# Four column groups of an output projection as seven block products each, with the heads' operand sums kept in DRAM

## The chip, the cores and the metric

The kernel runs on one core of a Trainium2 chip. TensorE (PE) multiplies 128x128 weight tiles with operands of up to 512 columns and adds up in PSUM. VectorE (DVE), ScalarE (ACT) and GpSimd (POOL) work beside it on SBUF and PSUM. Transfers are issued by SyncE (SP) and by POOL, each on a queue of its own that is worked off in order, and carried by the core's 16 DMA engines. The metric is the device time of one execution in microseconds, the median of three runs: 2347.07 us before the change (2345.48 to 2347.75).

## The reference

One layer of a hybrid streaming encoder on 512 prompt frames and 32 sample frames (T = 544 columns here, since the kernel keeps features on partitions). What matters:

```python
x   = layer_norm(x) @ w_in                      # 2048 -> 4928
o_h = rms_norm(hgrn2_recurrence(q, 1 - f, log f, i)) * silu(g)    # 8 heads of 128
o_a = mla_attention(...)                                          # 8 heads of 128
out = concat([o_h, o_a]) @ w_out                # 2048 -> 2048
h   = layer_norm(ALPHA * h + out)
ff  = (silu(conv(h @ w_up)) * (h @ w_gate)) @ w_down
y   = layer_norm(ALPHA * h + ff)
```

Everything is float32.

## The kernel before, in words

**Products.** A float32 product is made from three products of rounded parts: each weight tile is split into a high part `wh` (ACT, a copy to the rounded type) and a low part `wl = raw - wh` (DVE), each operand likewise into `aH` and `aL`, and PE adds wh·aH, wh·aL and wl·aH (`mm3`). A matmul has 128 rows, 128 columns of weight and 272 columns of operand: T is halved into columns 0 to 271 (j = 0) and 272 to 543 (j = 1). A weight piece is 128x1024 (512 KB): four 128-row blocks by 256 output columns. It serves 48 matmuls when both halves of T are done, 24 for one half.

**Seven products.** Where a matrix product is cut into 2x2 blocks, the kernel can form it from seven block products in place of eight (`ORDER`: 11, s1, s2, s4, s3, 12, 22), with sums of weight blocks as weights and sums of operand blocks as operands. The later two thirds of the input projection (class `Divided`, L788) and the feed-forward layer (classes `Blocks` and `Item`, played by `play`, L1257 and L1288) are done so. `play` walks a list of items: it multiplies item n, splits the weights of item n+2 (`prep`) and forms the weight sum of item n+3 (`form`); the result of item n-1 is added from PSUM in its `sink`.

**Around the change.** In order of time: the attention heads (`attend`, results into DRAM tiles `cat_dr`); the recurrence of eight heads woven into the divided input projection (`levels(h)` and `finish(h)`, which ends in the head's output `o`); then `out_first`, which loads and splits all 16 heads into `cH`, `cL` and makes output columns group 0 (256 columns) as a plain product while the last head is finished; then groups 1 to 4 as plain products of both halves (`gemm`, 192 matmuls each); groups 5 and 6 with half 0 only (`gemm_half`, 96 matmuls each); group 7's half 0 and half 1 of groups 7, 5 and 6 in `step`, with the first norm's work between the steps (`TASKS`).

**The first norm.** `h0` (the normalised input) is loaded back from DRAM into `za` (features 0 to 7, on POOL's queue) and `zb` (8 to 15, on SP's queue). `z = ALPHA * z + product`. Behind group 0 `Norm.first` takes a first estimate of the row means, for each half j: DVE `n_e = za0 + za1`, PE sums of one column (`sums`), DVE `nt_c`, PE spreads them over the partitions (`spread`), ACT `n_cb`. From then on every block of z is made as ALPHA*z - cb (`shifted`) and has the product added (`joined`); row sums and sums of squares are carried along (POOL `n_s`, ACT `n_e`, DVE `n_s`).

**Order.** Inside `manual_schedule` blocks each engine's order is the program's. The part from `finish` of the last head to group 6 is not in such a block: there the framework decides the order of the instructions of each engine from its own estimate of when they can run. Pools give out buffers in rings (`raw` three, `wh` and `wl` four), and a buffer is written again when its readers are through.

Of the kernel before, what the change touches and what calls it, by code (L numbers as in the profile page):

```python
# [9 lines left out]
I32 = mybir.dt.int32  # L10
# [36 lines left out]
HK = 8  # L47
# [12 lines left out]
def tile_encoder_step(ctx, tc, xp, xs, w_in, w_in4, w_kr, w_q_b, w_kv_b, w_out, w_up, w_gate, w_down, w_down2,  # L60
# [14 lines left out]
    cat_dr = [dram.tile([P, 2, T], F32, name=f"catd{k}", tag=f"catd{k}") for k in range(KD // 2)]  # L75

# [17 lines left out]

    def load_raw(src, kc, ncols):
        raw = wp.tile([P, 1024], F32, name="raw", tag="raw", bufs=3)[:, :kc * ncols]
        dma(raw, src)
        return raw.rearrange("p (k c) -> p k c", k=kc)
# [49 lines left out]
    def pair_half(ps, j):  # L148
        n = H_[j].stop - H_[j].start
        return [ps[:, 512 * t:512 * t + n] for t in range(2)]  # L150

# [46 lines left out]
    with tc.tile_pool(name="p0", bufs=1) as p0, tc.tile_pool(name="ps0", bufs=4, space=PSUM) as ps0:  # L198
# [12 lines left out]
        def load_first(kk):  # L211
            for g in range(2):
                raws[kk, g] = p0.tile([P, 4, 256], F32, name="raw0", tag="raw0", bufs=5) if g or kk == 3 else \
                    wp.tile([P, 1024], F32, name="raw", tag="raw", bufs=3).rearrange("p (k c) -> p k c", k=4)
# [149 lines left out]
    with tc.tile_pool(name="mp", bufs=1) as mp, tc.tile_pool(name="psa", bufs=4, space=PSUM) as psa:  # L364
# [208 lines left out]
        def attend(pr):  # L573
# [58 lines left out]
            dma(cat_dr[4 + pr], o)  # L632

# [8 lines left out]
    def out_piece(kk, g):  # L642
        return piece(w_out[kk, g], 4, 256)
# [12 lines left out]
    with tc.tile_pool(name="gp", bufs=1) as gp, tc.tile_pool(name="psg", bufs=1, space=PSUM) as psg:  # L656
        hm = gp.tile([P, T + 272 * 6], I32, name="hm")
# [19 lines left out]
        def sums_of_inputs():  # L677

            load_sums()
            for k in range(HK):  # L680
# [9 lines left out]
                V.tensor_tensor(out=a, in0=t0, in1=t1, op=ALU.subtract)  # L690
                V.tensor_tensor(out=b, in0=t1, in1=t1b, op=ALU.add)
                V.tensor_tensor(out=c, in0=b, in1=t0, op=ALU.subtract)
# [3 lines left out]
                V.tensor_tensor(out=a, in0=t0b, in1=c, op=ALU.subtract)  # L696
# [8 lines left out]

        class Divided:


            def __init__(self, c):
                self.c, self.raw = c, {}  # L710

            def load(self, key):
                if key == "21":
                    self.raw[key] = gp.tile([P, HK * P], F32, name="raw21", tag="raw21")
                else:
                    self.raw[key] = wp.tile([P, 1024], F32, name="raw", tag="raw", bufs=3)
                dma(self.raw[key], w_in4[self.c - N_PLAIN, int(key[0]) - 1, int(key[1]) - 1])

            def form(self, name):
                if name == "11":  # L720
                    for key in ("11", "12", "22", "21"):
                        self.load(key)
                r = self.raw
# [619 lines left out]
    for name in ("11", "12"):  # L1343
        open_op(name, apx, "right")
# [1047 lines left out]
```

## Time and profile before

| | us |
|---|---|
| median of three runs | 2347.07 |
| the profiled execution, its own time | 2347.67 |
| span of its trace | 2345.9 |
| PE busy in the span | 2305.4 |
| mean granted clock of PE | 0.994 |

| stage | from, to (us of the span) |
|---|---|
| divided input projection with the recurrence | 383 to 701 |
| output columns group 0 | 701.4 to 730.4 |
| groups 1 to 4 | 730.4 to 832 |
| groups 5 and 6, half 0 | 832 to 856.5 |
| group 7, halves 1, first norm | 856.5 to 907 |
| feed-forward layer and last norm | 907 to 2346 |

How to read the rows: an engine's row in a timeline has its start, its length, the engine, the line of the kernel, the operation, the tile written and the tiles read, and in brackets how long the engine was idle before it and what released it. A table of stretches gives for each engine the busy time and the number of instructions, then PE's granted clock (1.00 is full), the busy share of the DMA engines and what they moved. A DMA row gives the number of transfers, KB of each and the median time from issue to landing.

### The profile page before, as it was taken

The numbers are of one execution on the slowest core, as the hardware profiler recorded it, in microseconds if no ns is written. First come the engines' busy times: TensorE is split into PE (matmuls) and PEld (weight loads), VectorE is DVE, ScalarE is ACT, GpSimd is POOL, SyncE is SP. The second block draws the span as 40 slices with busy tenths as digits, with TensorE's granted clock in tenths as the row PEclk, the third lists the DMA queues.
The fourth block names the chain that finished last, engine by engine and source line by source line (L and its number), as shares of the span: only waits on it lengthen the run. The fifth ranks groups of instructions, "written<-read, shape, count | busy, mean of one in ns | idle before, by whom it ended". The sixth has DMA issues, their size and how long they took to land.

```text
span 2345.9 us, 44466 instructions
## 1 busy us (share of the span) xinstructions
PE 2305.4 (98%) x18340; PEld 2289.3 (98%) x18340; DVE 1703.1 (73%) x2357; ACT 1075.3 (46%) x1652; POOL 221.4 (9%) x277
## 2 busy tenths in 40 slices
PE   7999999999999999999999999999999999999996
PEld 6999999999999999999999999999999999999996
DVE  7455578777786358987777777777777677777776
ACT  5345434433352227665555554555555433333323
POOL 1010000000001111000010000100001111111102
PEclk9999999999999999999999999999999999999998
DMA  6332263222245236777677676776777999889832
GB/s 238 104 99 84 69 205 104 86 93 82 81 144 194 91 109 210 217 203 207 201 179 227 176 198 208 176 230 177 190 216 190 371 325 303 270 277 299 286 94 79
DMA packets 155963, 427.47 MB, mean 182 GB/s; under 512 B 14192, under 2 KB 70256, under 8 KB 148464
## 3 DMA queue, kind: packets, MB, share of 16 engines
q1 hardware_dynamic: 129488, 302.20, 37.4%
q0 software_dynamic: 26272, 122.43, 21.8%
q8 instruction: 144, 2.36, 0.4%
q14 instruction: 59, 0.48, 0.1%
HBM read 351.75 MB, written 70.11 MB: 180 GB/s over the span
## 4 chain that ended last, share of the span: by engine, by line
PE 95%; DVE 1%; ACT 1%; DMA 1%; issue 1%; POOL 0%; ACTq 0%; SPq 0%; DVEq 0%
PE main L1257 22%; PE acc L1257 17%; PE main L118 13%; PE main L788 11%; PE main L1288 11%; PE acc L1288 7%; PE acc L118 5%; PE s L853 2%; PE main L555 1%; PE at L616 1%; PE at L585 1%; DMA x<-in_xp 1%; PE main L542 0%; PE at L587 0%; DMA raw<-in_w_in 0%
## 5 line engine op out<-in xcount | busy, mean ns | idle before, releaser
L1199 DVE TENSOR_TENSOR wl<-raw,wh 128x1024 fp32r<-128x1024 f32 x353 | 431.9, 1223 | 192.5 <-ACT wh L1198 192.2
L1198 ACT ACTIVATE wh<-raw 128x1024 fp32r<-128x1024 f32 x353 | 373.2, 1059 | 388.0 <-PE main L1257 99.2
L1257 PE MATMUL main<-op,wh 128*128 128x272 f32 x1408 | 265.4, 287 | 0.0
L1257 PE MATMUL acc<-ops,wh 128*128 128x272 f32 x1344 | 254.1, 287 | 0.0
L1257 PE MATMUL main<-ops,wh 128*128 128x272 f32 x1344 | 254.1, 287 | 0.0
L1257 PEld LDWEIGHTS main<-op,wh 128*128 128x128 f32 x1408 | 221.0, 188 | 0.0
L1257 PEld LDWEIGHTS acc<-ops,wh 128*128 128x128 f32 x1344 | 211.1, 188 | 0.0
L1257 PEld LDWEIGHTS main<-ops,wh 128*128 128x128 f32 x1344 | 211.0, 188 | 0.0
L1257 PE MATMUL main<-op,wl 128*128 128x272 f32 x704 | 202.9, 288 | 0.3 <-DVE wl L1199 0.3
L1257 PE MATMUL main<-ops,wl 128*128 128x272 f32 x672 | 193.7, 288 | 0.0
L1257 PE MATMUL acc<-ops,wl 128*128 128x272 f32 x672 | 193.7, 288 | 0.0
L118 PE MATMUL main<-aH,wh 128*128 128x272 f32 (+2 forms) x736 | 176.5, 296 | 0.2 <-ACT wh L280 0.2
L118 PE MATMUL main<-aH,wl 128*128 128x272 f32 (+2 forms) x736 | 172.7, 291 | 1.8 <-DVE wl L281 1.8
L118 PE MATMUL main<-aL,wh 128*128 128x272 f32 (+2 forms) x736 | 172.3, 291 | 1.0 <-DVE aL L269 1.0
L1257 PE MATMUL acc<-op,wh 128*128 128x272 f32 x832 | 157.5, 288 | 1.0 <-ACT ea L1511 1.0
L1198 ACT ACTIVATE wh<-rawl 128x1024 fp32r<-128x1024 f32 x93 | 98.9, 1063 | 118.4 <-PE acc L1257 45.8
L107 DVE TENSOR_TENSOR wl<-raw,wh 128x1024 fp32r<-128x1024 f32 (+2 forms) x72 | 80.2, 1117 | 89.6 <-ACT wh L106 85.6
L732 ACT ACTIVATE wh<-raw 128x1024 fp32r<-128x1024 f32 x84 | 88.7, 1056 | 111.4 <-DVE raw L727 105.1
L1199 DVE TENSOR_TENSOR wl<-rawl,wh 128x1024 fp32r<-128x1024 f32 x93 | 113.8, 1223 | 27.7 <-ACT wh L1198 27.6
L1257 PEld LDWEIGHTS main<-op,wl 128*128 128x128 f32 x704 | 132.2, 188 | 0.5 <-DVE wl L1199 0.5
L1257 PEld LDWEIGHTS acc<-op,wh 128*128 128x128 f32 x832 | 130.4, 188 | 1.2 <-ACT ea L1511 1.2
L1257 PEld LDWEIGHTS main<-ops,wl 128*128 128x128 f32 x672 | 126.3, 188 | 0.0
(448 smaller groups left out, 5998.0 us busy)
## 6 DMA issues: line engine op xcount, KB each, us to landing
raw<-in_w_in SPq DMA_DIRECT2D x76, 512.0 KB, 3.6
raw<-in_w_up SPq DMA_DIRECT2D x71, 512.0 KB, 4.9
raw<-in_w_gate SPq DMA_DIRECT2D x71, 512.0 KB, 4.8
raw<-in_w_down SPq DMA_DIRECT2D x67, 512.0 KB, 9.4
opd<-ohl SPq DMA_DIRECT2D x20, 1088.0 KB, 5.5
ops<-opd POOLq DMA_DIRECT2D x20, 1088.0 KB, 12.0
raw<-in_w_out SPq DMA_DIRECT2D x40, 512.0 KB, 3.6
raw<-in_w_up POOLq DMA_DIRECT2D x35, 512.0 KB, 5.3
```

What stands on the lines that cost most here:

```text
L107: V.tensor_tensor(out=dst(lv), in0=src(rv), in1=dst(hv).bitcast(F32), op=ALU.subtract)
L118: PE.matmul(ps, ww[:, wcols[0]:wcols[1]], aa[:, hs[j]], start=first and i == 0, stop=last and i == 2, skip_group_check=True)
L555: PE.matmul(ps[:, j * 512:j * 512 + 256], l[k][:, a:b], r4(w[:, k:k + 1, :])[:, 0, :, 128:256], start=k == 0 and i == 0, stop=k == 1 and i ...
L585: PE.matmul(sc[:, :nk], qn[j][:, q0:q0 + P], kn[j][:, :nk], start=True, stop=False)
L616: PE.matmul(po[:, :P], vt[:, k, j, :], t[:, k * P:(k + 1) * P], start=k == 0, stop=k == b)
L732: A.activation(wh, self.src, AF.Copy)
L788: PE.matmul(out, ww[:, k * P:(k + 1) * P], aa, start=name in ("11", "s1", "12") and k == 0 and q == 0, stop=k == HK - 1 and q == 2, skip_g ...
L853: PE.matmul(ps[:, j * 64:(j + 1) * 64], Kp[:, a:b], Qv[:, j * bt:(j + 1) * bt, 1, :], start=True, stop=True)
L1198: A.activation(wh, src, AF.Copy)
L1199: V.tensor_tensor(out=wl, in0=src, in1=wh.bitcast(F32), op=ALU.subtract)
L1257: PE.matmul(ps, ww[:, k * P:(k + 1) * P], aa, start=self.first and k == 0 and i == 0, stop=k == n - 1 and i == 2, skip_group_check=True)
L1288: PE.matmul(banks[:, 512 * u:512 * u + NI], ww[:, (u * n + k) * P:(u * n + k + 1) * P], aa, start=self.first and k == 0 and i == 0, stop=k ...
```

## The change

Output column groups 1 to 4 (features 256 to 1279) become seven block products each, from weights that are laid out in 2x2 blocks (`w_out4`). A block has 1024 rows by 128 columns, so one product is 24 matmuls, and the four groups are 28 items of class `Out`. They are played by `play`, first products 11 and 12 of all four groups, then for each group s1, s2, s4, s3, 22.

The operands of 11, 12 and 22 are halves of the heads themselves (`cH`, `cL`). Those of s1, s2, s3 and s4 are sums over pairs of a recurrence head and an attention head. `finish(h)` forms them for its head, while the recurrence runs, in high and low parts, and stores them in DRAM (`ou_dr`, four stores of 278 KB for each head); for that `attend` leaves the difference of its output's halves in DRAM (`d3_dr`). s1, s2 and s4 are loaded back into `su` (six loads of 1088 KB on POOL's queue). s3 is placed over the second halves of the attention heads in `cH`, `cL` (`place_s3`), after these have been copied to DRAM (`a21_dr`, 16 stores on POOL's queue); they are loaded back behind the last s3 product (`place_a21`, 16 loads on SP's queue).

The order of the groups changes: group 0, then groups 5 and 6 half 0, then the 28 items, then group 7 as before.

In the recurrence `Divided` makes its weight sums by two DVE additions and two accumulating DMAs on POOL's queue for each group, where there were four DVE subtractions; the signs of the operand sums and of the results change with that. The mask `hm` becomes 8-bit. Buffers `raw` have tags of their own.

```diff
@@ finish, behind the head's output o
+            hl = {}
+            def high(name, x):
+                hl[name] = gp.tile([P, 2, NI], R, name="hl", tag="hl", bufs=2)
+                A.activation(hl[name][:, 0], x, AF.Copy)
+            def low(name, x):
+                V.tensor_tensor(out=hl[name][:, 1], in0=x, in1=hl[name][:, 0].bitcast(F32), op=ALU.subtract)
+                dma(ou_dr[name][h // 4][:, :, h % 4], hl[name].bitcast(F32))
+            yield
+            minus(ab[:, 0], o[:, NI:], ab[:, 0])
+            high("s3", ab[:, 1])
+            yield
+            low("s3", ab[:, 1])
+            high("s1", ab[:, 0])
+            opposite(ab[:, 1], ab[:, 1], o[:, NI:])
...
+            low("s4", ab[:, 1])
@@ Divided
             def form(self, name):
-                        V.tensor_tensor(out=r[out], in0=r[a], in1=r[b], op=ALU.subtract)
+                if name in ("s1", "s2"):
+                    other = {"s1": "12", "s2": "22"}[name]
+                    V.tensor_tensor(out=self.t("11"), in0=self.t("11"), in1=self.t(other), op=ALU.add)
+                if name == "s1":
+                    G.dma_start(self.t("12"), self.src("22"), accum_op=ALU.add)
             def low(self, wh):
+                if self.name == "s2":
+                    G.dma_start(self.t("11"), self.src("21"), accum_op=ALU.add)
+                elif self.name not in ("11", "s1"):
+                    slots.append(self.raw.pop(self.key)[0])
+                    supply()
@@ out_first, split_cats
+                    if k >= HK:
+                        for n, t in enumerate((cH[k], cL[k])):
+                            G.dma_start(a21_dr[k - HK][:, n], t[:, NI:].bitcast(F32))
@@ behind the loads of za and zb
+    for n in ("s1", "s2", "s4"):
+        for i in range(2):
+            G.dma_start(su[n][i].bitcast(F32), ou_dr[n][i])
@@ groups
-    for g in range(1, 5):
-        tiles = [acc_tile(), acc_tile()]
-        run(gemm(tiles, lambda kk: out_piece(kk, g), cact, CAT_ORDER))
...
-    for g in (5, 6, 7):
+    for g in (5, 6):
...
+    class Out(Item):
+        def operand(self, k):
+            if self.name in su:
+                return [su[self.name][k // 4][:, i, k % 4] for i in range(2)]
+            kg, j = {"11": (HK + k, 0), "12": (k, 0), "22": (k, 1), "s3": (HK + k, 1)}[self.name]
+            return cH[kg][:, H_[j]], cL[kg][:, H_[j]]
+        def multiply(self):
+            wh, wl = self.w
+            for k in range(HK):
+                oh, ol = self.operand(k)
+                for i, (ww, aa) in enumerate(((wh, oh), (wh, ol), (wl, oh))):
+                    PE.matmul(self.bank, ww[:, k * P:(k + 1) * P], aa, start=self.first and k == 0 and i == 0,
+                              stop=k == HK - 1 and i == 2, skip_group_check=True)
...
+        def out_sink(g, name, ps):
+            t, j = PLACE[name]
+            z = zt[2 * g + t][:, H_[j]]
+            if (g, t, j) in touched:
+                V.tensor_tensor(out=z, in0=z, in1=ps, op=SIGN[t])
+            else:
+                touched.add((g, t, j))
+                V.scalar_tensor_tensor(out=z, in0=z, scalar=ALPHA, in1=ps, op0=ALU.mult, op1=SIGN[t])
+            if name in ("s4", "22"):
+                close_rows(g, 0 if name == "s4" else 1)
...
+        for g in range(1, 5):
+            for name, key, bank in (("11", "11", X[g]), ("12", "21", BC[g % 2])):
+                oitems.append(out_item(out_blocks(g, (key,)), g, name, bank, True))
+        for g in range(1, 5):
+            b = out_blocks(g, ("11", "12", "22"))
+            oitems += [out_item(b, g, name, BC[(g + 1) % 2] if name in ("s1", "s4") else X[g])
+                       for name in ("s1", "s2", "s4", "s3", "22")]
...
+        ohooks = {0: [lambda: place_s3(range(4))], 1: [lambda: place_s3(range(4, 8))],
+                  NO - 2: [lambda: split_seventh(0)],
+                  NO - 1: [place_a21, lambda: split_seventh(1), lambda: [shifted(14 + t, 0) for t in range(2)]]}
+        play(oitems, 0, ohooks)
```

Since the framework orders this place anew, here are the rows of three engines there, before and with the change.

DVE, from the last head's output (`og`, split into `aL`) to the first norm's second half, before:

```order
L177 TENSOR_TENSOR aL<-og,aH 128x544
L1397 SCALAR_TENSOR_TENSOR za<-za,main 128x272 x4
L1059 TENSOR_TENSOR n_e<-za 128x272
L107 TENSOR_TENSOR wl<-raw,wh 128x1024
L1065 TENSOR_SCALAR nt_c<-main 128x3
L1076 TENSOR_TENSOR za<-za,n_cb_8319 128x272
L1077 TENSOR_TENSOR za<-za,n_cb_8319 128x272
L1356 SCALAR_TENSOR_TENSOR za<-za,n_cb_8319 128x272 x2
L1086 SCALAR_TENSOR_TENSOR n_s_8322<-n_e 128x272
L1356 SCALAR_TENSOR_TENSOR za<-za,n_cb_8319 128x272
L1059 TENSOR_TENSOR n_e<-za 128x272
```

With the change:

```order
L991 TENSOR_TENSOR hl<-ab,hl 128x272 x2
L167 SCALAR_TENSOR_TENSOR ab<-ab,og 128x272
L118 TENSOR_TENSOR wl<-raw,wh 128x1024
L991 TENSOR_TENSOR hl<-ab,hl 128x272
L1451 SCALAR_TENSOR_TENSOR za<-za,main 128x272 x4
L1124 TENSOR_TENSOR n_e<-za 128x272
L1128 TENSOR_SCALAR nt_c<-main 128x3
L1134 TENSOR_TENSOR za<-za,n_cb_8550 128x272
L1135 TENSOR_TENSOR za<-za,n_cb_8550 128x272
L1410 SCALAR_TENSOR_TENSOR zb<-zb,n_cb_8550 128x272 x2
L1141 SCALAR_TENSOR_TENSOR n_s_8553<-n_e 128x272
L1410 SCALAR_TENSOR_TENSOR zb<-zb,n_cb_8550 128x272
```

The low part of a weight piece (`wl`), which stood behind `n_e`, now stands ahead of the four `za`, with a low part `hl` of an operand sum; the shifted blocks behind `n_cb` are of `zb` in place of `za`, and the second half's `n_e` comes right behind the last row shown.

PE, from the last matmuls of group 0 to the second half's sums, before:

```order
L118 MATMUL main<-aH,wl 128x272 x2
L1048 MATMUL main<-ones,n_e 128x1 x3
L118 MATMUL main<-aH,wh 128x272 x2
L118 MATMUL main<-aL,wh 128x272 x2
L118 MATMUL main<-aH,wl 128x272 x2
L118 MATMUL main<-aH,wh 128x272 x2
L118 MATMUL main<-aL,wh 128x272 x2
L1053 MATMUL main<-ident,nt_c 128x128 x2
```

With the change:

```order
L129 MATMUL main<-aH,wl 128x272 x2
L1113 MATMUL main<-ones,n_e 128x1 x3
L129 MATMUL main<-aH,wh 128x272
L1118 MATMUL main<-ident,nt_c 128x128 x2
L1118 MATMUL main<-ident,nt_c 128x16
L129 MATMUL main<-aL,wh 128x272
L129 MATMUL main<-aH,wl 128x272
```

Ten matmuls lay between the sums and the spread, now one; 24 more lay between the spread and the second half's sums, now 18 (each for one half of T).

SP's queue around the loads of `zb`, before (`raw` are the next weight pieces):

```order
L905 DMA out_stp<-S 128x128
L97 DMA raw<-in_w_out 128x1024 x2
L1353 DMA zb<-h0d_77 128x544
L1353 DMA zb<-h0d_78 128x544
L1353 DMA zb<-h0d_79 128x544
```

With the change:

```order
L941 DMA out_stp<-S 128x128
L108 DMA raw<-in_w_out 128x1024 x2
L992 DMA ous_98<-hl 256x1x272
L992 DMA ous_100<-hl 256x1x272
L108 DMA raw<-in_w_out 128x1024
L992 DMA ous_104<-hl 256x1x272
L1401 DMA zb<-h0d_77 128x544
L1401 DMA zb<-h0d_78 128x544
```

Three stores of operand sums (s1, s2, s4 of the last head) and one more weight piece now stand ahead of the `zb` loads.

More of the change, by code (lines that the diff above doesn't have):

```diff
@@ L150, in pair_half, with minus, opposite @@
         return [ps[:, 512 * t:512 * t + n] for t in range(2)]
+    def minus(out, a, b):
+        V.tensor_tensor(out=out, in0=a, in1=b, op=ALU.subtract)
+    def opposite(out, a, b):
+        V.scalar_tensor_tensor(out=out, in0=a, scalar=-1.0, in1=b, op0=ALU.mult, op1=ALU.subtract)
     def run(*gens):
@@ L642, in out_piece @@
     def out_piece(kk, g):
-        return piece(w_out[kk, g], 4, 256)
+        return piece(w_out[kk, max(g - 4, 0)], 4, 256)
     cH, cL = {}, {}
@@ L688, in two @@
                     V.tensor_tensor(out=l, in0=x, in1=h.bitcast(F32), op=ALU.subtract)
-                V.tensor_tensor(out=a, in0=t0, in1=t1, op=ALU.subtract)
-                V.tensor_tensor(out=b, in0=t1, in1=t1b, op=ALU.add)
-                V.tensor_tensor(out=c, in0=b, in1=t0, op=ALU.subtract)
+                minus(a, t0, t1)
+                minus(b, t1b, t1)
+                opposite(c, b, t0)
                 two(a, s3[:, 0], s3[:, 1])
@@ L704, in place_s3, with supply @@
                     dma(t[k][:, H_[1]].bitcast(F32), s3_dr[k][:, i])
+        slots = [(wp, f"raw{n}") for n in range(3)] + [(gp, "raw21")]
+        waiting = []
+        def supply():
+            while waiting and slots:
+                g, key = waiting.pop(0)
+                p, tag = slots.pop(0)
+                t = p.tile([P, HK * P], F32, name="raw", tag=tag, bufs=1)
+                dma(t, g.src(key))
+                g.raw[key] = (p, tag), t
         class Divided:
@@ L959, in tile_encoder_step @@
         place_s3()
-        products[0][0].form("11")
+        supply()
         for n in range(2):
@@ L1644, in step @@
+    ou_stack.close()
+    st_stack, st = stack(pool("st", "right"))
+    with tc.manual_schedule():
+        for name in ("11", "12"):
+            x1_op[name] = [op_tile(name, i) for i in range(2)]
         def step(outs, w, j, kk):
@@ L1659, in tile_encoder_step @@
         again = [(kk, g) for g in (5, 6) for kk in ko]
-        raws = [load_raw(w_out[kk, g], 4, 256) for kk, g in again[:3]]
+        raws = [load_raw(w_out[kk, g - 4], 4, 256) for kk, g in again[:3]]
         ws = []
@@ L1833, in tile_encoder_step @@
         FIRST = ("11", "s1", "s2", "s3", "22")
-        SIGN = (ALU.add, ALU.subtract)
         def add_part(q, name, ps):
```

188 lines of the change are left out of this document (120 added, 68 removed).

## The prediction

> **What bounds the kernel now.** I read the page's engine line and its chain of waits first, then the table of stretches around the output projection, then the chain in order of time.
>
> ```profile
> PE 2305.4 (98%) x18340; PEld 2289.3 (98%) x18340; DVE 1703.1 (73%) x2357; ACT 1075.3 (46%) x1652; POOL 221.4 (9%) x277
> PE 95%; DVE 1%; ACT 1%; DMA 1%; issue 1%; POOL 0%; ACTq 0%; SPq 0%; DVEq 0%
> 383.00:700.00 317.00, 317.00 (x2605) 315.70 (x2604) 249.67 (x407) 133.33 (x197) 7.01 (x6) 1.00 0.30 95
> 730.50:742.50 12.00, 10.86 (x75) 10.68 (x75) 8.28 (x21) 2.83 (x7) 0.91 (x2) 0.86 0.84 322
> 742.50:856.50 114.00, 114.00 (x913) 114.00 (x912) 55.37 (x74) 31.08 (x42) 20.05 (x19) 1.00 0.32 102
> 856.50:907.00 50.50, 50.50 (x408) 50.50 (x407) 37.37 (x53) 27.46 (x41) 6.53 (x7) 1.00 0.38 122
> ```
>
> TensorE (PE) is the bound: 98% busy and 95% of the chain. The rows by stretch (columns: length, busy PE, PEld, DVE, ACT, POOL, granted clock, DMA share, GB/s) say that it never pauses in the divided recurrence (383 to 700), nor in groups 1 to 6 (742.5 to 856.5), where VectorE (DVE) is only 55.37/114 = 49% busy. The one weak place near the change is the seam behind group 0, 730.5 to 742.5: busy 10.86 of 12 and a clock of 0.86. So a matmul removed is worth its own time, as long as the engines that feed the PE keep up, and the seam must be looked at singly.
>
> ```profile
> 724.36 6.06 PE main L118 x48
> 730.42 0.02 issue
> 730.45 0.51 DVE za L1397 x2
> 730.96 0.19 issue
> 731.15 0.45 DVE n_e L1059
> ```
>
> **The matmuls removed.** 48 matmuls of 128x272 take 6.06 us here at full clock, 0.126 us each. Four groups at 4 pieces x 48 = 768 become 28 products x 24 = 672: 96 fewer, **-12.0 us**, all on the path, since these stretches are PE without a pause. Groups 5 and 6 keep their matmuls.
>
> **The seam behind group 0.** In both kernels the three one-column sums of the first norm half stand directly behind group 0 in the PE's order, and wait for DVE's n_e. What stands ahead of n_e on DVE differs (order lists above). The rows of the timeline now:
>
> ```profile
> 730.25 1.06 ACT L106 ACTIVATE wh<-raw 128x1024 fp32r<-128x1024 f32 x1 [4.24 <-PE main L118]
> 731.50 1.22 DVE L107 TENSOR_TENSOR wl<-raw,wh 128x1024 fp32r<-128x1024 f32 x1
> 731.64 0.83 PE L1048 MATMUL main<-ones,n_e 128*128 128x1 f32 x6 [1.23 <-DVE n_e L1059]
> 734.02 1.29 PE L1053 MATMUL main<-ident,nt_c 128*128 128x128 f32 x6
> 735.36 0.40 ACT L1070 ACTIVATE n_cb<-main 128x272 f32<-128x272 f32 x1 [4.05 <-PE main L1053]
> 735.79 0.44 DVE L1076 TENSOR_TENSOR za<-za,n_cb 128x272 f32<-128x272 f32 x1 [3.00 <-ACT n_cb L1070]
> 739.07 0.80 PE L1048 MATMUL acc<-ones,n_e 128*128 128x1 f32 x6
> 740.32 0.73 PE L1053 MATMUL acc<-ident,nt_c 128*128 128x128 f32 x6
> ```
>
> Before, wl of the fourth prefetched piece runs behind n_e; now it runs ahead of it, with a low part hl and all four za. That wl needs its wh, which ACT can only start at 730.25 (its ring of four is freed by the PE). So: wh ends 731.3; wl 1.2 to 732.6; hl 0.36; four za at 0.36 (a pair lasts 0.79 busy by the rows, 0.36 apart); n_e 0.43: the sums start at 734.9 instead of 731.64, 3.3 us later, all of it PE idle.
>
> What an idle PE does to the clock is in the trace at three places, cut into 3.4 us stretches:
>
> ```profile
> 149.60:153.00 3.40, 2.58 (x17) 2.30 (x16) 3.22 (x4) 1.41 (x3) 0.65 (x2) 1.00 0.38 116
> 367.20:370.60 3.40, 2.48 (x20) 2.29 (x20) 3.40 (x7) 1.69 (x2) 0.00 (x0) 1.00 0.51 142
> 370.60:374.00 3.40, 3.40 (x30) 3.40 (x29) 1.61 (x2) 2.33 (x4) 0.00 (x0) 1.00 0.47 176
> 729.80:733.20 3.40, 2.17 (x18) 1.95 (x18) 2.35 (x5) 1.06 (x1) 0.00 (x0) 1.00 1.03 395
> 733.20:736.60 3.40, 3.40 (x18) 3.40 (x17) 0.81 (x3) 0.73 (x2) 0.00 (x0) 0.50 1.06 389
> ```
>
> 0.92 us idle (367.2) left the next stretch at 1.00; 1.23 us idle (729.8) put the whole next stretch at 0.50, which costs 1.7 us. I take it that over about 1.2 us of idle time in one such stretch halves the next. The Trainium skill ("TensorE: Matmul & The Clock Gate", section "HAM oscillation — how this bites in real kernels") would have only gaps above some 3.4 us drop the clock. The 1.23 us row speaks against it; by the page the second gap below would cost no clock, and the sum would be 1.7 us better.
>
> Now walk on. 733.2 to 736.6 is at half clock again, and 736.6 to 740.0 too, since the stretch before it holds 1.7 us of idle time. Sums 734.9; spread 1.25 later as the second time (739.07 to 740.32), since one matmul instead of ten now covers that chain: 736.15 to 737.45 at half clock. n_cb and the first za follow as in the rows (1.8 us from spread start): 737.9. DVE then has two za, three zb, one n_s and n_e, 2.6 us: 740.5. The PE has 18 matmuls before the second sums: ten at half clock to 740.0, eight at full, 741.0. By then 19 matmuls (2.4 us) are done in the 10.6 us since 730.4, so 8.2 are lost; before, 34 (4.3 us) were done in 8.66, 4.4 lost. **+3.8 us**, if nothing else is late.
>
> But those three zb (rows of h0 times ALPHA minus the mean) need the third to fifth zb load, and n_e of the second half stands behind them on DVE, with the PE behind n_e. Those loads moved on SP's queue: they stand behind a further weight piece, which waits for the same wl (732.6), and behind the store of the last operand sum (hl, 733).
>
> ```profile
> 726.85 5.89 SPq L1353 DMA_DIRECT2D zb<-h0d  x8
> DMA to landing us min/median/max: 5.8/6.9/7.6
> cx<-catd SPq DMA_DIRECT2D x3, 272.0 KB, 3.1
> raw<-in_w_down SPq DMA_DIRECT2D x5, 512.0 KB, 13.8
> ops<-opd POOLq DMA_DIRECT2D x1, 1088.0 KB, 14.2
> ```
>
> First issue about 733.8 instead of 726.85, 0.74 apart, the fifth at 736.8. Landing took 5.8 to 7.6 us with the DMA full (rows above at 389 to 395 GB/s), 3.1 for the same size on an emptier DMA around 700, and 13.8 for 512 KB pieces while 1088 KB operand loads ran on POOL's queue (1875 to 1895). After the change POOL's queue has six such 1088 KB loads; five wait for the last sum's store, so most start behind the zb issues. I take 5.8: lands 742.6, n_e ends 743.5, the PE idles 2.5 us from 741.0 and the next stretch is halved: **+2.5 +1.7**. Bounds: 0 (3.1), and 10.5 plus 3.4 of clock (13.8).
>
> **The products themselves.** Per group of five products (15.0 us of PE) DVE now has 5 wl, 2 weight sums, 5 sinks, 2 wide subtractions and 4 additions of squares:
>
> ```profile
> L107 DVE TENSOR_TENSOR wl<-raw,wh 128x1024 fp32r<-128x1024 f32 x23 | 29.8, 1297 | 50.9 <-ACT wh L106 50.5
> L1099 DVE TENSOR_TENSOR n_s<-n_s,n_e 128x272 f32<-128x272 f32 x18 | 13.3, 770 | 0.9 <-ACT n_e L1095 0.8
> L1361 DVE TENSOR_TENSOR za<-za,acc 128x272 f32<-128x272 f32 x6 | 2.4, 435 | 1.3 <-PE acc L118 1.3
> L1090 POOL TENSOR_TENSOR n_s<-n_s,za 128x272 f32<-128x272 f32 x12 | 12.6, 1074 | 55.6 <-issue 55.6
> raw<-in_w_up POOLq DMA_DIRECT2D x35, 512.0 KB, 5.3
> ```
>
> 7 x 1.22 to 1.30 + 5 x 0.44 + 2 x 0.72 (estimate: an aL of twice 272 columns) + 4 x 0.67 to 0.77 = 14.9 to 15.8 us against 15.0. Rows are busy times that overlap at their ends (a wl passes DVE on after 1.13), so some 13.5; DVE goes from 49% to about 90%. Weights are split two products (6 us) ahead, which absorbs the bursts behind s4 and 22; I take 0.7, bounds 0 and 4 x (15.8 - 15.0) = 3.2. The accumulating weight DMA has three products (9 us) against two POOL additions (2.1), 0.9 of issue and 5.3 of landing: 8.3, hidden; if it were 3 us later it would show.
>
> **Edits that I cost at little.** In the recurrence, two of four weight subtractions per group become accumulating DMAs (-2 x 1.22 on DVE), and each head's sums add seven DVE operations of 272 (about 2.5 us), four on ACT and six transfers: per head -4.9 + 2.5 on DVE under a PE that never waits (317.00 of 317.00): 0. The first head's sums have no such cover, since around 367 to 371 DVE is 3.40 of 3.40 busy and PE idles 0.92: 0 to 2.5, I take 0.5. Behind the products, 16 loads put the attention heads' second halves back, at 0.74 of SP issue each 11.8 us, begun one product (3 us) early, while the 96 matmuls of group 7's first half run 12.0: covered by 3 us, less a landing of 3.1; 0 to 2, I take 0.3.
>
> **Sum.** -12.0 + 3.8 + 4.2 + 0.7 + 0.5 + 0.3 = -2.5 us on the profiled execution's 2347.67: 2345.2. That execution lies 0.6 above the median of the runs, so **2344.6 us**.
>
> **Rivals.**
> *The seam stays short* (0.22): zb lands in about 3 us, or DVE finds za earlier. For it: POOL's large loads mostly wait. Against it: the DMA ran at 389 GB/s there. -12.0 + 3.8 at most and little else: 2335 to 2340.5, at 2338.9.
> *DVE paces the products* (0.15): 15.8 against 15.0 per group and the chain of n_e, square and addition behind s4 and 22 in order. Against it: 6 us lead. +3.2 and the first head's 2.5 instead of 1.2: 2349.
> *The zb loads starve behind POOL's operand loads* (0.15, slower): 13.8 us of landing instead of 5.8 adds 8 us of idle time and one more half-clock stretch: 2344.6 + 9.7 = 2354. It decides from about 5.5 us more landing on. For it: the rows at 1875; against it: the loads' own waits.
> The forecast, most of the gain given back at the seam, 2340.5 to 2349, has 0.48.
>
> **Numbers.** About 0.2% (4.7 us) can be told from no change, so faster ends at 2342.4. Faster: 0.22 + 0.15 of the forecast = 0.37; slower: 0.15 + 0.02 of the second rival = 0.17; the same 0.46. The range runs from the shortest seam, 2336, to 2353, which leaves out part of the starved case and the case of no seam cost at all.
>
> **What would show it.** Right: two PE waits behind group 0 in the list of waits, one of about 4.5 us and one of 1 to 5 us on n_e, with granted clock 0.50 around 733 to 740; products at 3.0 us each; first zb issue at about 734. Wrong: sums within 2 us of group 0's end; a list of PE waits on wl inside the products adding up to over 3 us; idle PE at 365 to 385 above 3 us; or any pause in the recurrence.

## The result, and the profile after

The changed kernel takes 2403.94 us (median of 4 runs, 2401.32 to 2405.06) beside 2347.01 us before (4 runs): the ratio is 1.0242, with a 95% interval of 1.0224 to 1.026. It is slower by 57 us, where 2344.6 and a range of 2336 to 2353 were predicted. The page of the profile after, its engine line and its chain of waits:

```profile
PE 2314.2 (96%) x18244; PEld 2294.8 (96%) x18244; DVE 1725.3 (72%) x2413; ACT 1095.3 (46%) x1696; POOL 272.7 (11%) x351
PE 86%; DVE 5%; DMA 4%; ACT 3%; issue 2%; SPq 0%; POOL 0%; ACTq 0%; DVEq 0%; POOLq 0%
```

The 96 matmuls are gone (x18340 before, x18244 now), yet PE is busy for 8.8 us longer: it runs more of its time at half clock. It fell from 95% to 86% of the chain, and DMA, which had 1%, now has 4%.

I cut both traces at the same four events (last matmul of the recurrence's projection, last matmul of group 0, first matmul of the items or of group 1, end of the part that the change touches):

| stage | before, us | after, us | difference | forecast |
|---|---|---|---|---|
| recurrence, its end at | 701.6 | 726.9 | +25.3 | +0.5 |
| group 0 | 28.9 | 28.9 | 0 | 0 |
| seam, groups 5 and 6 half 0 | 29.8 | 56.0 | +26.2 | +8.0 |
| groups 1 to 4 | 96.3 | 101.0 | +4.7 | -11.0 |

Groups 5 and 6 cost 192 matmuls x 0.1254 us (96.3 / 768) = 24.1 us in both kernels; before the change they stand behind groups 1 to 4, and are put with the seam here so that like stands beside like (before: 126.1 from 730.4 to 856.5, less 96.3 for 768 matmuls). The sum of the differences is +56.2, against 56.7 between the two spans. So all three stages missed the forecast, by 24.8, 18.2 and 15.7 us.

**The recurrence.** Stretches of the kernel after (length, busy PE, PEld, DVE, ACT, POOL, granted clock, DMA share, GB/s):

```profile
383.00:700.00 317.00, 305.36 (x2462) 303.30 (x2462) 227.03 (x395) 127.39 (x199) 26.68 (x28) 0.98 0.54 141
400.00:420.00 20.00, 18.56 (x141) 18.34 (x140) 12.01 (x24) 6.89 (x11) 0.00 (x0) 0.91 0.63 175
520.00:540.00 20.00, 16.57 (x125) 16.47 (x125) 11.88 (x26) 5.66 (x9) 0.00 (x0) 0.91 0.62 184
700.00:720.00 20.00, 15.81 (x106) 15.62 (x106) 11.23 (x25) 8.86 (x16) 3.24 (x6) 0.83 0.85 299
```

Where the same 317 us were full before (x2605), PE now does 2462 matmuls, and there is a hole in about one of every three stretches of 20 us: once a head. DVE is busy for less time than before (227 of 317 us, 249.67 before), in part because less was done in that time, so it is not short of time here. What ACT waits for between 380 and 720, and its row at the end of one such wait:

```profile
ACT hl L988 <- DMA ous<-hl: 52.9, 8, 9.7
```

```profile
467.09 0.43 ACT L988 ACTIVATE hl<-ab 128x272 fp32r<-128x272 f32 x1 [8.66 <-DMA ous<-hl]
467.43 1.04 ACT L760 ACTIVATE wh<-raw 128x1024 fp32r<-128x1024 f32 x1
468.37 0.38 ACT L806 ACTIVATE hproj<-main 128x272 f32<-128x272 f32 x1
```

`finish(h)` rounds four operand sums one after the other into a ring of two buffers (`hl`, bufs=2). The third sum can be rounded only when the first has been stored, and in the chain of waits between 452 and 475 that store (272 KB in the profile's units, the 278 KB of the description) stands with 6.45 us:

```profile
460.09 0.36 DVE hl L991
...
460.54 6.45 DMA ous<-hl
...
467.09 0.43 ACT hl L988
467.52 0.95 ACT wh L760
```

ACT works in order, so the next weights' high part (`wh`) and the copy of a finished projection out of PSUM (`hproj`), which have nothing to do with the sums, stand behind the waiting copy, and PE behind them. It waited for `hproj` and for the recurrence's own `Kp`:

```profile
PE acc L1113 <- DVE n_e L1124: 13.7, 1, 13.7
PE main L1704 <- DVE za L1734: 9.7, 3, 3.3
PE main L821 <- ACT hproj L806: 9.6, 4, 3.4
PE main L1113 <- DVE n_e L1124: 8.0, 1, 8.0
PE s L886 <- DVE Kp L892: 6.6, 5, 4.2
```

These are the five largest PE waits of the changed kernel that the kernel before did not have, or had only at 1.2 us (the fourth); the numbers are us in total, times, longest. The third and fifth are the recurrence, the second is inside the block products, the first and fourth are the seam.

**The seam.** The chain of waits there, after:

```profile
753.10 0.44 ACT hl L988
...
753.68 7.17 DMA ous<-hl
...
760.96 0.44 ACT hl L988
761.40 0.02 issue
761.42 0.45 DVE hl L991
...
765.16 21.98 DMA zb<-h0d
...
787.16 0.44 DVE zb L1410
```

The last head's last sum waits for the same ring (7.17 us), and its low part `hl` stands on DVE ahead of the four `za` and of `n_e`: the first wait is 8.0 us. The issue rows show what follows: the last sum also releases the `us` operand loads on POOL's queue, the first at 762.50 and the other five from 765.15, in the very moment at which SP gets to the `zb` loads.

```profile
762.46 4.42 SPq L1401 DMA_DIRECT2D zb<-h0d  x8
```

```profile
762.50 0.53 POOL L1407 DMA_DIRECT2D us<-ous  x1 [8.38 <-DVE hl L991]
765.15 2.67 POOL L1407 DMA_DIRECT2D us<-ous  x5 [2.12 <-issue]
```

With six loads of 1088 KB beside them, a `zb` load of 272 KB takes up to 22 us to land, and PE waits 13.7 us for the second `n_e`. The granted clock was 0.61 from 760 to 780 and 0.71 from 780 to 800.

**The products.** The chain of waits at the end of group 1's products, after:

```profile
846.15 0.45 DVE za L1734
...
846.62 0.74 DVE za L1725
...
847.38 0.44 ACT n_e L1150
...
847.85 0.74 DVE n_s L1154
...
849.43 1.22 DVE wl L1247
...
850.68 1.22 DVE raw L1257
851.90 0.36 DVE za L1734
...
852.39 4.78 PE main L1704 x24
```

Products s3 and 22 stand next to each other and share a PSUM bank (`X[g]`), so 22 starts only when s3's sink (851.90) has read it. That sink stands on DVE behind s4's sink (846.15), its wide subtraction, two additions that wait for squares on ACT, a `wl` and a weight sum. The wait stands there three times, for 3.3, 3.2 and 3.2 us. The product behind the first two took 4.8 and 4.6 us where 24 matmuls take 3.0 (half clock); behind the third it took 3.1, at full clock. At full clock 672 matmuls x 0.1254 are 84.3 us, so 16.8 of the 101.1 us are lost: PE is idle for 11.3 (busy 89.8 of 101.1), the two stretches of half clock cost 3.4, and 2.1 are left, which also stand in the last kernel below, where the clock was 1.00 (busy 86.3).

### The profile page after: what moved, and what is told of

The parts are those of the page before. It is cut to its first block, busy times and chain, and to the rows that moved or that the text cites. A ratio compares the mean times of both kernels' runs of the same rounds, so it can differ in the third digit from the quotient of the medians.

```text
span 2402.6 us, 44712 instructions
## 1 busy us (share of the span) xinstructions
PE 2314.2 (96%) x18244; PEld 2294.8 (96%) x18244; DVE 1725.3 (72%) x2413; ACT 1095.3 (46%) x1696; POOL 272.7 (11%) x351
## 4 chain that ended last, share of the span: by engine, by line
PE 86%; DVE 5%; DMA 4%; ACT 3%; issue 2%; SPq 0%; POOL 0%; ACTq 0%; DVEq 0%; POOLq 0%
PE main L1305 21%; PE acc L1305 16%; PE main L129 10%; PE main L1336 10%; PE main L821 7%; PE acc L1336 7%; PE acc L129 3%; DMA ous<-hl 2%; PE main L1704 2%; PE acc L1704 1%; PE s L886 1%; DMA zb<-h0d 1%; DVE wl L765 1%; PE main L572 1%; PE at L633 1%
## 5 line engine op out<-in xcount | busy, mean ns | idle before, releaser
L1247 DVE TENSOR_TENSOR wl<-raw,wh 128x1024 fp32r<-128x1024 f32 x373 | 456.0, 1223 | 200.7 <-ACT wh L1246 200.5
L1246 ACT ACTIVATE wh<-raw 128x1024 fp32r<-128x1024 f32 x373 | 393.8, 1059 | 407.8 <-PE main L1305 99.0
L129 PE MATMUL main<-aH,wh 128*128 128x272 f32 (+2 forms) x608 | 150.7, 299 | 0.4 <-ACT wh L297 0.2
L129 PE MATMUL main<-aH,wl 128*128 128x272 f32 (+2 forms) x608 | 148.3, 295 | 2.7 <-DVE wl L298 1.8
L129 PE MATMUL main<-aL,wh 128*128 128x272 f32 (+2 forms) x608 | 148.1, 295 | 1.0 <-DVE aL L286 1.0
L765 DVE TENSOR_TENSOR wl<-raw,wh 128x1024 fp32r<-128x1024 f32 x84 | 102.8, 1224 | 59.6 <-ACT wh L760 58.6
L1247 DVE TENSOR_TENSOR wl<-rawl,wh 128x1024 fp32r<-128x1024 f32 x93 | 113.7, 1223 | 26.2 <-ACT wh L1246 26.1
L821 PE MATMUL main<-s,wh 128*128 128x272 f32 x576 | 118.5, 303 | 9.6 <-ACT hproj L806 9.6
```

Of the source, the lines that this page charges most:

```text
L129: PE.matmul(ps, ww[:, wcols[0]:wcols[1]], aa[:, hs[j]], start=first and i == 0, stop=last and i == 2, skip_group_check=True)
L765: V.tensor_tensor(out=wl, in0=self.t(self.key), in1=wh.bitcast(F32), op=ALU.subtract)
L821: PE.matmul(out, ww[:, k * P:(k + 1) * P], aa, start=name in ("11", "s1", "12") and k == 0 and q == 0, stop=k == HK - 1 and q == 2, skip_g ...
L1246: A.activation(wh, src, AF.Copy)
L1247: V.tensor_tensor(out=wl, in0=src, in1=wh.bitcast(F32), op=ALU.subtract)
```

## The experiments

Each kernel computes the whole layer. The edits are to the changed kernel; "before" measured 2346.2 to 2347.0 us beside them. A time without a range is that of a single run.

**Layout of the stored sums.**

```diff
-dram.tile([P, 2, 4, NI], F32, name=f"ou{n}{i}", ...)      # 1088-byte runs
+dram.tile([P, 4, 2, NI], F32, name=f"ou{n}{i}", ...)      # 2176-byte runs; all readers likewise
```

> The operand sums lie in DRAM as [128, 4 heads, 2 parts, 272] instead of [128, 2 parts, 4 heads, 272], so that a store of one head writes 2176 bytes in a row for each partition instead of twice 1088. Nothing else moves on PE, DVE, ACT or POOL. Theory (the stores land too late for a ring of two buffers): with the change a store took 5.5 us to land (median of 32) where the head's output of the same 272 KB takes 2.4; the landing should fall to 2.5 to 3.5, PE's waits in the recurrence (9.6 on ACT hproj, 6.6 on DVE Kp) to under 6 in all, the recurrence's end from 726.6 to about 708, and the time from 2404 to about 2380. Rival (eleven more operations for each head on ACT and DVE are too many, whenever the stores land): the waits and the time stay, 2400 to 2406.

2385.2 us. The times from issue to landing of the 32 stores, of the changed kernel and of this one:

```profile
DMA to landing us min/median/max: 2.5/5.5/7.6
```

```profile
DMA to landing us min/median/max: 2.0/5.4/6.7
```

The theory that short runs make the stores slow is refuted: twice the run length, the same landing. The recurrence's pauses stay (waits for `hproj` 8.3 us in total). The time came near the theory's 2380 all the same, but not in the way it named. The recurrence ended at 721.3, as it does in the next experiment, which leaves the layout alone. What did change is the seam: the `zb` loads went out from 754.88, 6.6 us ahead of five of the six `us` loads, landed in 13.5 us at most, and the second wait fell from 13.7 to 3.8. That this came from the layout is not shown, since the two queues' moments there depend on small delays.

**Closing the half behind s3.**

```diff
-            if name in ("s4", "22"):
-                close_rows(g, 0 if name == "s4" else 1)
+            if name in ("s3", "22"):
+                close_rows(g, 0 if name == "s3" else 1)
```

> The subtraction of the mean and the sums of a group's first half come behind the sink of s3 instead of behind the sink of s4. Theory (PE's product 22 adds to the bank that s3's sink still has to read, and on DVE that sink stands behind this work): the three waits of 3.3 us (9.7) fall to under 1 us each, the half-clock stretch behind each of them (4.8 us for a product instead of 3.0) goes too, and the time falls from 2404 to about 2390. Rival (DVE has too much work for 15 us a group): the waits turn up at wl or at another sink, and the time stays above 2400.

2389.18 us. The waits of 22 for `za`:

```profile
PE main L1704 <- DVE za L1734: 5.0, 3, 2.1
```

So s4's closing work ahead of s3's sink is about half of that wait. The half clock behind the waits went too: the clock of the items is 1.00, and they take 91.8 us instead of 101.1. That is 9.3 of the 14.8 us; the other 5.6 are not from the edit. The recurrence, which it doesn't touch, ended at 721.3 here and in the first experiment, at 726.9 in the changed kernel and 726.2 in the next one: its pauses are not the same in each build.

**The `zb` loads on POOL's queue, ahead of the `us` loads.**

```diff
-            (G.dma_start if k < HK else dma)(zt[k], h0_dr[k])
+            G.dma_start(zt[k], h0_dr[k])
```

> The eight zb loads are issued on POOL's queue behind the za loads, so ahead of the six operand loads of 1088 KB, instead of on SP's queue. Theory (zb loads share the DMA engines with the operand loads, 22 us to landing): they land before 766, the second half's n_e does not wait for them, PE's wait of 13.7 us falls below 3, and the time falls from 2404 to about 2386. Rival (the wait comes from the order at the seam, with wl and hl ahead of za, and only shows at zb): the wait of 13.7 us falls by less than half and the time stays above 2396.

2385.72 us. The wait of 13.7 us is gone from the list. The times from issue to landing of the `zb` loads, of the changed kernel and of this one:

```profile
DMA to landing us min/median/max: 8.1/17.8/22.1
```

```profile
DMA to landing us min/median/max: 3.7/6.6/8.2
```

They went out from 752.14 to 758.99 here, ahead of the first `us` load at 762.55. The first wait is 8.7, the items' waits 9.7 and the recurrence's end 726.2, as in the changed kernel. So the 13.7 us were the operand loads that ran beside the `zb` loads. The Trainium skill ("DMA: Bandwidth & Descriptors", section "Queues, rings and completion order") says that each DMA engine takes turns between the queues that have work; landings of 22 us beside the other queue's 1088 KB loads and of 8.2 ahead of them agree.

**All three.**

> The three edits together. Theory (three independent losses of about 24, 14 and 18 us): 2404 - 56 = 2348, within 6 us of the kernel before, and below it only if the seam's first wait (8.0 us, of which 4 are a store's landing) goes as well. Rival (the losses cover one another, or one pace-setter stands behind all three): 2365 or more.

2377.31 us (2375.26 to 2377.91), ratio 1.0131 (1.0114 to 1.0148); 29 us above what was expected. The recurrence again ended at 726.8, with 9.2 us of waits for `hproj` and 5.2 for `Kp`: nothing in the three edits touches the cause there, and the 721 us of the first two had been a chance of the build, not a gain. The first wait at the seam was still 7.8. The items took 91.7 us at a clock of 1.00, so the gain of the later closing came again.

**Own buffers for two of the four sums.**

```diff
-                hl[name] = gp.tile([P, 2, NI], R, name="hl", tag="hl", bufs=2)
+                if name in ("s3", "s1"):
+                    hl[name] = gp.tile([P, 2, NI], R, name="hl", tag="hl", bufs=2)
+                else:                       # s2, s4: the space of tiles that the head has done with
+                    tag = {"s2": "sqg", "s4": "vT"}[name]
+                    t = gp.tile([P, 5 * P], R, name="hl" + name, tag=tag, bufs=1)
+                    hl[name] = t[:, :2 * NI].rearrange("p (i c) -> p i c", i=2)
```

> The changed kernel with one edit: the operand sums s2 and s4 of a head are written to two buffers that are idle by then (those of the squares and of the transposed values), so that none of a head's four sums waits for the store of another one. Operations, orders and transfers stay. Theory (ACT works in order, and its rounding for s2 and s4 waits for a store that lands 5.5 us after its issue, with the next weights' rounding behind it): ACT's nine waits on these stores (57.3 us) go, PE's waits inside the recurrence (16 us) fall below 4, the recurrence ends at 703 to 708 instead of 726.6, the seam's first wait (8.0) falls to about 4.5, and the time falls from 2404 to about 2378. Rival (the added work on ACT and DVE itself, or transfers that share the DMA engines): the waits on the stores go but PE still waits over 10 us in the recurrence, and the time stays above 2394.

2371.43 us. From 400 to 700 PE is busy for 300.00 of 300.00 us, and the seam's waits fell with it, to 3.9 and 2.1: the ring was behind both. One new wait stands at the first head, since `vT` of the next head now waits for that store:

```profile
PE main L1709 <- DVE za L1739: 9.7, 3, 3.3
PE s L931 <- ACT vT L926: 5.8, 1, 5.8
PE main L1118 <- DVE n_e L1129: 3.9, 1, 3.9
```

The recurrence ended at 710.5: 16.3 of the 25.3 us are back, and the rest was lost between 365 and 395, where PE is idle for 6.9 us (0.9 before) and the clock is 0.89.

**The ring and the three.**

> The three earlier edits (row layout, later closing of a half, zb behind za on POOL's queue) with the four separate buffers. Theory (ring): 2377 - 22 in the recurrence - 4 at the seam = about 2351. Rival: 2370 or more.

2360.94 us, 10 above what was expected. The recurrence ended at 709.5, 17 earlier and not 22, since the wait at the first head is there again (5.0). The first wait at the seam is 3.9. The items' waits for s3's sink are 4.8, and the items took 94.6 us where the three edits alone had 91.7.

**Own buffers for heads 1 to 7 only.** Nothing of the seam or of the items is touched.

```diff
-                if name in ("s3", "s1"):
+                if name in ("s3", "s1") or h == 0:
```

> The changed kernel with the four separate buffers for heads 1 to 7 only; head 0 keeps the ring of two. Theory (in the run with separate buffers for all heads PE waited 5.8 us for vT around 380, because the second head's transposed values come while the first head's sum s4 is still being stored from that buffer): that wait and its half-clock stretch go, the recurrence ends at about 702 as in the kernel before instead of 710.5, and the time is about 2371 - 9 = 2362. Rival (the first heads lose that time to the added work in any case): it ends at 708 or later and the time stays above 2367.

2364.84 us, near the theory's 2362. The recurrence in this kernel (a table of stretches), three stretches at its seam, its largest PE waits from 725 to 800, and SP's issue rows:

```profile
383.00:700.00 317.00, 317.00 (x2606) 315.69 (x2605) 241.75 (x429) 141.50 (x223) 31.84 (x38) 1.00 0.62 162
...
741.60:745.00 3.40, 1.30 (x7) 1.33 (x7) 1.59 (x4) 0.00 (x0) 0.00 (x0) 0.71 1.01 411
745.00:748.40 3.40, 2.72 (x12) 2.40 (x13) 0.51 (x2) 0.18 (x1) 0.00 (x0) 0.50 1.01 417
748.40:751.80 3.40, 3.40 (x17) 3.40 (x17) 2.85 (x4) 1.89 (x4) 0.78 (x1) 0.50 1.03 427
```

```profile
PE main L1118 <- DVE n_e L1129: 3.9, 1, 3.9
PE acc L1118 <- DVE n_e L1129: 2.7, 1, 2.7
PE acc L1123 <- DVE nt_c L1133: 0.7, 1, 0.7
```

```profile
733.42 0.33 SPq L108 DMA_DIRECT2D raw<-in_w_out  x1
733.80 3.82 SPq L1406 DMA_DIRECT2D zb<-h0d  x8
```

317.00 of 317.00, as before the change, with the sums, the stores and the accumulating DMAs all in place: only the two-buffer ring cost anything in the recurrence. Its last projection matmul ends at 701.6, the same as before. And the seam is now the one that was forecast: sums at 735.19 (734.9 forecast), first `zb` issue at 733.80 (733.8), second wait 2.7 (2.5). From 734.8 to 755.2 the clock of six stretches of 3.4 us was 0.71, 0.79, 0.71, 0.50, 0.50 and 0.79; the rows shown are the second wait and what follows it. The seam lost 10.8 us to the kernel before (40.6 us less 24.1 is 16.5 here, 5.7 there), and the items lost 5.7 (102.0 against 96.3), so about 17 us stay.

**A different order of the products, with the ring and the three.** 11 of all groups first, then for each group s1, s2, s4, s3, 12, 22; half 0 is closed behind 12.

> As the one before, and product 12 of each group stands between s3 and 22 instead of ahead of all groups (products of one group: s1, s2, s4, s3, 12, 22), so that no product follows at once on one whose sum its own bank still holds. Theory (each product that adds to a bank waits for DVE to have read the one before): PE's remaining waits in the 28 products (4.9 us and up to 4 us of half clock) fall below 1, the 28 products take 84 to 86 us, and the time falls by 5 to 9 from the one before, to about 2344. Rival (DVE's work for a group is too much for 15 or 18 us): the waits move to wl and the time stays.

2358.41 us (2356.46 to 2360.68), ratio 1.0051 (1.0036 to 1.0066). That is 14 above what was expected. The waits for s3's sink are gone, but the items still took 92.8 us. Their waits came back at other sinks (3.5, 1.4 and 0.7), and part of that is a wait for weight pieces now, which landed in 7.8 and 7.5 us at 754 and 765.

**The seam's order written out by hand.** On top of the former: the two halves' sums directly behind each other, four blocks of group 5's matmuls ahead of the two spreads, and three of group 5's pieces split ahead of them.

```diff
+    with tc.manual_schedule(engines=MANUAL):
+        ...
+                    firsts.append(nrm[j].first(zt[0], zt[1], acc_tile()))
+                    next(firsts[j])
+        ...
+                    if n == 4:
+                        next(firsts[0])
+                        next(firsts[1])
```

> As the one before, and the seam behind group 0 written out by hand: the four za, both n_e, both halves' sums on PE, then the fourth weight piece's low part, twelve matmuls, both spreads; nothing of zb ahead of them. Theory (order at the seam): PE's wait behind group 0 falls from about 4.5 to about 1 us and the second one goes, one half-clock stretch remains or none; the time falls by 6 to 10, to about 2336, below the kernel before by 8 to 12. Rival (za or the DMA is late anyway): no more than 3 us.

2359.76 us (2357.2 to 2360.88), ratio 1.0053 (1.0036 to 1.007), where 2336 was expected: no gain. The seam's waits did go, from 3.9 to 1.4. But the largest PE waits of this kernel near it, and its longest piece of the chain:

```profile
PE main L1734 <- DVE za L1767: 7.8, 2, 7.2
```

```profile
761.27 13.20 DMA raw<-in_w_out
```

Groups 5 and 6 now run through without a pause, so the items begin sooner, while the six `us` loads still run, and a weight piece of 512 KB takes 13.2 us to land (414 GB/s from 760 to 780). From the end of the recurrence to the first item it is 4.3 us less than in the former, and the items took 97.8, 5.0 more: the time went from the seam to the DMA.

**The operand loads spread out.** On top of the former: first head's ring left alone, and the loads of s2 and s4 issued on SP's queue behind the first products, between their weight pieces.

```diff
-    for n in ("s1", "s2", "s4"):
-        for i in range(2):
-            G.dma_start(su[n][i].bitcast(F32), ou_dr[n][i])
+    for i in range(2):
+        load_su("s1", i, G.dma_start)
...
+        for n, (name, i) in zip((0, 0, 1, 1), (("s2", 0), ("s2", 1), ("s4", 0), ("s4", 1))):
+            ohooks.setdefault(n, []).append(lambda name=name, i=i: load_su(name, i))
```

> As the run with the seam written out (row layout, zb behind za, order 12 between s3 and 22, own buffers), with the separate buffers from head 1 on, and with the loads of the operands s2 and s4 (four of 1088 KB) on SP's queue between the weight pieces of the first products instead of on POOL's queue at the seam. Theory (the weight pieces landed 7 to 13 us after issue while six operand loads ran, and PE waited 7.8 us for the first products' chain): pieces land within 7 us, that wait falls below 2, and with the 8 us of the first heads the time falls from 2359.8 to about 2344. Rival (the DMA engines are full from 740 to 780 whatever the order): the wait stays above 5 and the time above 2349.

2350.41 us (10 runs, 2348.83 to 2353.08), ratio 1.0016 (1.0007 to 1.0025): 6 us short of what was expected, and just above the rival's 2349, with one wait of 4.0 us for weights left (chain at 782: a piece of 7.98).

**The change's own order again, spread out.** As the former, with 11 and 12 of all four groups first, and the loads behind items 0, 1, 3 and 4. The expectation names the closing behind s4; in the kernel it stands behind s3.

> As the one before, but with the change's own order of the 28 products (11 and 12 of all groups first; closing of a half behind s4). Theory: 12 us more for the operand loads, but the three waits of 3.3 us with their half-clock stretches are back: about 10 above the one before, 2354. Rival (the room for the loads is worth more): equal or faster than the one before.

2346.39 us (10 runs, 2344.3 to 2349.96), ratio 0.9999 (0.9989 to 1.0009): the rival's time came true. Its reason, the room for the loads (the eight first products need no stored sum, so the loads have 24 us there), is not shown: three edits lie between this kernel and the former (the order, the place of the closing, the pace of the loads), and they were not separated. Left inside the items (92.3 us) are the bank's waits:

```profile
PE main L1736 <- DVE za L1766: 3.9, 3, 2.1
```

**Something between s3 and 22.** In groups 1 to 3, 22 changes places with the next group's s1, whose bank is another.

```diff
+        for n in (12, 17, 22):
+            oitems[n:n + 2] = oitems[n + 1], oitems[n]
```

> The kernel of e11_paced_12first with one thing changed: in groups 1 to 3 the product 22 stands behind the next group's s1, so that a product with another PSUM bank lies between s3 and 22, which share one. What is left in e11 between 780 and 900 us are three waits for s3's sink (3.9 us together, longest 2.1) and two stretches at a granted clock of 0.96 and 0.95 (about 1.8 us). Theory (the bank that s3's sink still reads holds 22 up, and nothing else does): PE waits of L1736 for za under 1 us together, clock 1.00 there, time 2346.4 - 5.7 = about 2341 (2339 to 2343). Rival (DVE, busy 16.4 to 16.6 of 20 us there, is what paces these groups; the wait is only where its lateness shows): the same 3 to 4 us come back as PE waits for wl, or for the sinks at another product, and the time stays at 2345 to 2348.

2341.94 us (10 runs, 2338.41 to 2343.98) beside 2346.98: ratio 0.9976 (0.9966 to 0.9985). This is faster than the changed kernel and, by 5 us, than the kernel before the change. The items of this kernel, and groups 1 to 4 of the kernel before the change:

```profile
763.40:852.80 89.40, 86.34 (x681) 85.46 (x680) 67.46 (x87) 32.89 (x43) 20.15 (x24) 1.00 0.75 215
```

```profile
730.50:826.80 96.30, 95.16 (x749) 94.98 (x750) 45.43 (x73) 22.91 (x34) 14.36 (x14) 0.98 0.34 117
```

The items take 89.4 us, 3 less than in the former kernel (92.3). The clock is 1.00 throughout and no wait for s3's sink ahead of 22 is left, but 2.5 us of waits for `za` are (longest 1.5), where the theory had under 1. The two longer ones are put down to 22's sink, which for the longest stands on DVE behind two weight splits: a small part of the rival holds too. They stand at the s2 of groups 2 and 4, though 22 was in another bank; the banks of groups 1 and 2, and of 3 and 4, lie in one PSUM tile, and at group 3's s2, where they don't, there is no such wait. Whether the shared tile is the reason was not tried. Of the 5.1 us above 84.3, PE is idle for 3.1 and busy for 2.1 more than 672 x 0.1254; that second part has no cause here. The seam costs 1.8 more than before the change, and the recurrence ends 1.3 later.

## Why the prediction was wrong

**The recurrence, "per head -4.9 + 2.5 on DVE under a PE that never waits (317.00 of 317.00): 0".** This is the step that failed first and most (+24.8). The sum priced DVE's operations and named a cover for them. It named the six transfers and ACT's four operations too but gave them no price, and the ring's two buffers don't appear in it. In its place the runs show ACT waiting 57.3 us in nine waits for the stores, with the weights' rounding behind it, and a recurrence that ends 25.3 us later. The step's own premise, that sums in place cost PE nothing, was right: with the ring relieved, 317.00 of 317.00 came back. The prediction named "any pause in the recurrence" as a sign that it is wrong, but had no rival for it. Two things stood there to be put together: bufs=2 for four tiles in a row in the change, and the landing of 5.8 to 7.6 us that the prediction itself quotes for 272 KB.

**The seam, "+3.8" and "+4.2".** The mechanism was right; its input was not. The sums were placed at 734.9, with `hl` 0.36 us ahead of `za`; that holds in the kernel with the ring relieved (735.19). In the changed kernel `hl` itself waited 7.17 us for a store, so the first wait was 8.0 and not 4.5. The second wait was priced at 2.5 with a landing of 5.8, on the ground that "most start behind the zb issues"; the last store's lateness brought both to the same moment (762.46 and 762.50). That is the rival of loads that starve behind POOL's: landings fell from 22.1 to 8.2 us at most when the `zb` loads stood ahead, and its price of 13.8 us of landing was too low. Its time, 2354, still rested on a free recurrence.

**Half clock.** The prediction's rule, that more than about 1.2 us of idle time in a stretch of 3.4 us halves the next, holds at the seam (2.7 us of wait, then 0.50) and behind two of the three waits of 22 (3.3 us, then 4.8 us for 24 matmuls). The Trainium skill ("TensorE: Matmul & The Clock Gate", section "HAM oscillation — how this bites in real kernels") states as its rule that there be no idle gaps above some 3.4 us; here gaps of 2.7 and 3.3 us already cost clock. But idle time alone doesn't decide, so the rule is not right as it stands. In the changed kernel the half clock begins at 409.3, 528.8, 586.8, 706.3, 760.9, 853.0 and 873.5, which is 35, 52, 87, 103, 130 and 136 steps of 3.413 us behind the first. In the step from 405.9 to 409.3 PE is idle for 1.44 us and the next step is at 0.50; in the step from 467.35 to 470.75 it is idle for 1.45 us and the next stays at 1.00, and so it does behind the third wait of 22, with 1.84 us idle from 890.6 to 894.0. In the step with 1.44 us, and in the one with 1.23 us that the rule was taken from, part of the busy time went to narrow matmuls (64 columns and 1 column); in the two that left the clock at 1.00 it all went to matmuls of 272 columns. That this makes the difference is not shown.

The size at the seam was too low: three stretches at half clock were forecast (5.1 us at 1.7 each), and in the kernel with the ring relieved the six stretches below full clock amount to four of them (6.8 us; 3.4 x the sum of what is missing to 1.00, some of it while PE was idle). A third wait of 0.7 for `nt_c`, which stands behind a fourth `zb`, was not in the sum. Together they come to at most 2.4 of the 2.8 us from +8.0 to +10.8.

**The products, "I take 0.7, bounds 0 and 3.2".** 16.8 us were lost. DVE's work was sized rightly: 53.6 us in the 20 products from 836.8 on, 13.4 a group, where some 13.5 were forecast. Weights, "split two products (6 us) ahead", were no cause either. What was left out is a wait that the order of banks makes: s3 and 22 in one bank, next to each other, and s3's sink behind six other DVE operations. A row for it could not stand in the trace before, but the table of banks is in the change. The two experiments on it halve the wait and end the half clock (closing later, 101.1 to 91.8 us), and take away what was left of the wait for s3's sink (a product between, 92.3 to 89.4). Of the gain of 12.0 us for the matmuls removed, 7 were reached: in the last kernel groups 1 to 4 cost 89.4 instead of 96.3.

**The loads that I costed at little.** The 16 `a21` loads at the end and the accumulating DMAs are named by no PE wait of the changed kernel. That was right.

**A slip in a rival.** The second rival puts the first head at "2.5 instead of 1.2"; the sum has 0.5 there. Its 2349 goes by the 0.5, so neither the forecast nor a chance hangs on it.

What stays open: why the recurrence of the changed kernel ends at 721 in some builds and at 726 in others, what besides idle time decides the clock, and how much of the 4 us between the two kernels with spread loads belongs to the order, to the place of the closing and to the pace of the loads.

## What to carry to other kernels

When a change adds stores from a ring of buffers, count the buffers against the tiles that come in a row, and price the wait of the third tile as the whole time from issue to landing; then list what else stands behind the waiting instruction on its in-order engine, since that is what PE feels. When products add into shared PSUM banks, look for neighbours with one bank, and put a product with another bank between them. And a stage that gets faster moves its loads into its neighbour's: 4.3 us won at the seam came back as a weight piece that took 13.2 us to land, until the loads were spread.

## What the runs showed of the hardware

A store of 272 KB lands in 2.4 us where it goes out alone (`catd<-og`) and in 5.5 (the `ous<-hl` stores, median) where two go out at once, mostly behind a weight piece on the same queue; runs of 2176 instead of 1088 bytes did not change that (5.4). The predicated copies took about as long with the 8-bit mask as with the 32-bit one before (578 against 590 ns for 128x272), so the smaller mask bought next to no time.
